# The seven products of a Strassen pair emitted ahead of their sums, the norm's scales behind the second pair, and attention's raw tiles in the ring of the output projection's weights

## The chip, the cores and the metric

The kernel runs on one core of a Trainium2 chip. The metric is the device time of one execution in microseconds (us). The kernel before takes 1793.49 us, the median of three runs (1792.94 to 1795.22). The engines named below are TensorE (PE, the matmuls; PEld is its weight load), VectorE (DVE), ScalarE (ACT), GpSimd (POOL) and SyncE (SP, which issues most of the DMAs).

## What is computed

One layer of a bidirectional hybrid encoder on a sequence of 1024 tokens with model width 1024, in float32. Cut to what matters here:

```python
h    = rms_norm(x, g1) @ W_in                  # one combined projection
cat  = concat[dilated-window attention (8 heads, 512 wide),
              bidirectional RWKV-7 (8 heads, 512 wide)]
x    = x + cat @ W_out                         # 1024 x 1024
h    = rms_norm(x, g2)                         # x / sqrt(mean(x^2) + 1e-6) * g2
x    = x + squared_relu(h @ W_up) @ W_down     # 1024 -> 4096 -> 1024
```

## The kernel before

**Matmuls.** Every large product is computed as three matmuls on rounded halves: `mm3` (L104-107) multiplies high by high (L105), high by low (L106) and low by high (L107) into one PSUM tile. `split_w` (L100-102) makes the halves of a raw tile: ACT casts it to the high half (L101, tiles `wuh`, `w2h`, `f`), and DVE subtracts that from the raw tile for the low half (L102, `wul`, `w2l`, `f`).

**Order.** The program is emitted in Python and a scheduler then sets the order of the instructions on each engine from its own model of their times, keeping the dependencies. So the order on an engine isn't the order of the code. Tiles come from pools with a fixed number of buffers; a tile that takes over a buffer waits until the last user of the one before is done. A DMA that SP issues blocks SP's later DMAs while it waits for its buffer.

**The end of the kernel** is `tail()` (L987-1237). Until about 1006 us attention's last pieces run beside it (`some`, L1013).

- *Output projection.* `w_out` (L1023) takes columns of W_out for a list of rows `ks` and an output block `c`, adds the product to `x1[c]` (L1038). First come rows 4 to 7 (the RWKV half and attention's last heads, L1041-1044) for all eight blocks, then row 0 (L1048), then rows 1 to 3 (L1062). Rows 0 to 2 are attention's results of earlier heads, which lie in device memory (`cat_dr`): `cat(k)` (L1018) loads one into a raw tile of 128x1024 (512 KB) and splits it into `f`. That raw tile comes from `raw4` (L1006), a ring of two buffers that the blocks of W_up use too, before and after. The weights' raw tiles `w2raw` (L1028) have a ring of three buffers in the pool `w0`.
- *MLP, up.* x1 is scaled by g2 only (`hraw`, L1071) and split into the seven right factors of a Strassen-Winograd scheme, `h11`, `h21`, `h22`, `hT1` to `hT4`, while rows 1 to 3 of `w_out` run. The norm's scale per token is not needed for these products, as it can be applied to their results. Two blocks of W_up make a pair (`up_unit`, L1157; 16 pairs): seven products "11", "21", "22", "T1" to "T4", each of 12 matmuls of 128x512 into a PSUM bank of its own (84 matmuls a pair; eight banks, pool `pu`). Their left factors come from `factors` (L1104): quarters of the raw blocks, or sums of them that POOL makes (`wus`, L1114, three buffers), each split into `wuh` and `wul` (four buffers). DVE makes the Winograd sums of the products (L1173, and L1195 for the first pair alone); `add` (L1168) emits each product together with its sum.
- *Norm.* `sums()` squares x1 on ACT (L1141, tile `sqt`) and adds the 16 squares up in `rep`, one half of the tokens on DVE, the other on POOL (L1142). `scales()` sums over the partitions with 16 small matmuls (`psr`, L1147), takes the square root on ACT (L110, with a load of the function table), the reciprocal on DVE (L111), spreads the result over the partitions with 8 matmuls (`psb`, L1153) and copies it back to `rep` on DVE (L1155).
- *Finish.* `finish(u)` (L1198) takes each of a pair's four results: ReLU and scale in one DVE instruction (L1200), square on POOL (L1201), and a DMA by POOL to device memory (`f_dr`, L1202).
- *MLP, down* (L1211-1237) reads `f_dr` back, splits it and adds to x1.

The first pair has an order of products of its own (11, 21, 22, T2, T3, T1, T4), with one more sum and one more copy (L1181-1184, L1193-1195); in the others it is 11, T2, T3, T1, 21, T4, 22. The code calls the first pair, the norm (`sums`, `scales`), `finish` of the first pair, and then pair after pair.

Of the kernel before, what the change touches and what calls it, by code (L numbers as in the profile page):

```python
# [16 lines left out]
P = 128  # L17
# [30 lines left out]
def tile_trunk(ctx: ExitStack, tc: tile.TileContext, xT, w_in, w_o, w_up, w_dn, vecs, w2w0, a2, g2, cst, att,  # L48
# [938 lines left out]
    def tail(pieces, left, rw, at, fps):  # L987
        with ExitStack() as st:
# [9 lines left out]
            o0 = ExitStack()  # L998
            c00 = o0.enter_context(tc.tile_pool(name="c00", bufs=1, side="right", reuse_waits="tile"))
            w0 = o0.enter_context(tc.tile_pool(name="w0", bufs=3, side="right", reuse_waits="tile"))  # L1000
# [17 lines left out]
            def cat(k):  # L1018
                raw = raw4(cat_dr[k].rearrange("p (k m) -> p k m", m=P)).rearrange("p k m -> p (k m)")
                for hf in range(2):  # L1020
                    split_w(raw[:, HS[hf]], fh[k][:, HS[hf]], fl[k][:, HS[hf]])

            def w_out(wp, ks, c):  # L1023
                ws = {}
                for i in range(0, len(ks), 3 if len(ks) == 3 else 2):
                    k = ks[i]
                    n = len(ks) if len(ks) < 4 else 2
                    raw = wp.tile([P, n, P], F32, name="w2raw", bufs=3)  # L1028
                    nc.sync.dma_start(raw, w_o[c][:, k:k + n])
                    w = [wp.tile([P, n, P], F32R, name=x) for x in ("w2h", "w2l")]  # L1030
# [10 lines left out]
            for c in range(NK):  # L1041
                nc.sync.dma_start(x1[c], xT[c * P:(c + 1) * P, :])
                w_out(w0, [4, 5, 6, 7], c)
                some(4)
# [59 lines left out]
            def factors(u):  # L1104
# [12 lines left out]
                if u == 0:  # L1117
                    yield halves(a12)
                s1 = summed(nc.gpsimd.tensor_add, a21, a22)
                s2 = summed(nc.gpsimd.tensor_sub, s1, a11)  # L1120
                if u == 0:
                    yield halves(summed(nc.gpsimd.tensor_sub, a12, s2))
# [3 lines left out]
                if u > 0:  # L1126
                    yield halves(a12)
                yield halves(a22)
                if u > 0:
                    yield halves(summed(nc.gpsimd.tensor_sub, a12, s2))  # L1130
# [25 lines left out]

            def up_unit(u):  # L1157
                w = factors(u)

                def prod(ps, q):  # L1160
                    wh, wl = next(w)
# [6 lines left out]
                def add(a, q, out):  # L1168

                    ps = acc()  # L1170
                    prod(ps, q)
                    for x, t in zip(a, out):
                        nc.vector.tensor_add(t, x, ps)  # L1173
                    return out
                ps = acc()
                prod(ps, "11")
                t1 = z("t", bufs=2)
                nc.scalar.copy(t1, ps)
                if u == 0:
                    z11, = add([t1], "21", [z("z")])  # L1180
# [157 lines left out]
```

## Time and profile before

| | |
|---|---|
| median of three runs | 1793.49 us |
| the profiled execution | 1798.4 us |
| its span, first to last instruction | 1796.5 us |
| PE busy, share of the span | 1630.6 us, 91% |
| DVE, ACT, POOL busy | 1030.1, 595.8, 420.4 us |
| mean granted TensorE clock | 0.932 |

The 1.9 us between the execution's time and its span lie around the first and the last instruction. Rows of a timeline give the start and the busy time of an instruction in us, the engine, the line, the operation, its output and input tiles with shapes, a count where like instructions follow each other, and in brackets the idle time of the engine just before and what ended it. Matmuls are pipelined, so the busy time of one is longer than the distance to the next.

### The profile page before, as it was taken

What the parts mean: (1) busy time and instruction counts of PE and PEld (TensorE: products, weight loads), DVE (VectorE), ACT (ScalarE), POOL (GpSimd) and SP (SyncE); (2) the same over time, 40 slices, a digit from 0 to 9 for tenths busy, and PEclk for the clock granted to TensorE, in tenths of its full rate; (3) what the DMA queues carried; (4) which work ended last, traced back from release to release, by engine and by line L of the source; (5) the groups of instructions that cost most, each with busy time, mean ns of one, the idle gap of its engine ahead of it and who ended that gap; (6) DMA issues with size and microseconds to landing.
All of it is one profiled execution on the core that took longest, in us unless ns stands there. A gap on an engine that the chain in (4) does not pass through costs nothing.

```text
span 1796.5 us, 29980 instructions
## 1 busy us (share of the span) xinstructions
PE 1630.6 (91%) x11720; PEld 1346.6 (75%) x11720; DVE 1030.1 (57%) x1949; ACT 595.8 (33%) x1092; POOL 420.4 (23%) x459
## 2 busy tenths in 40 slices
PE   7999978879869897989997997699999999999999
PEld 6777767767657777877786885588888778788887
DVE  6655658657554423565765577677877744242421
ACT  5534433344412213435464334322222222131310
POOL 3022121222200000221223125566666500000000
PEclk9999988889879997988997998799999999999999
DMA  7155787879874689997972501133333343241421
GB/s 220 43 141 133 155 165 171 172 170 186 193 172 124 184 207 219 263 270 200 248 195 85 197 24 36 53 110 119 106 110 113 123 147 117 71 140 47 141 94 47
DMA packets 338157, 256.66 MB, mean 143 GB/s; under 512 B 238912, under 2 KB 292048, under 8 KB 333920
## 3 DMA queue, kind: packets, MB, share of 16 engines
q1 hardware_dynamic: 301632, 212.60, 45.4%
q0 software_dynamic: 8704, 26.78, 4.9%
q10 hardware_dynamic: 27680, 15.38, 3.2%
q8 instruction: 92, 1.51, 0.4%
q14 instruction: 49, 0.40, 0.1%
HBM read 167.00 MB, written 87.69 MB: 142 GB/s over the span
## 4 chain that ended last, share of the span: by engine, by line
PE 63%; DMA 14%; DVE 11%; SPq 5%; ACT 4%; issue 3%; POOL 1%; ACTq 0%; DVEq 0%; POOLq 0%
PE ps L105 12%; PE ps L106 12%; PE ps L107 12%; PE ps_u L105 3%; PE ps_u L106 3%; PE ps_u L107 3%; DMA v_dr<-vn 2%; PE pvb L748 2%; PE psd L564 2%; PE psg L496 2%; DMA rec<-rec_dr 1%; DMA raw<-f_dr 1%; PE ps_pt L742 1%; DVE stmp L534 1%; DMA MP<-gd 1%
## 5 line engine op out<-in xcount | busy, mean ns | idle before, releaser
L105 PE MATMUL ps<-mh,wuh 128*128 128x512 f32 x512 | 199.6, 391 | 4.5 <-ACT mh L101 3.2
L106 PE MATMUL ps<-ml,wuh 128*128 128x512 f32 x512 | 199.8, 390 | 2.1 <-DVE ml L102 2.1
L107 PE MATMUL ps<-mh,wul 128*128 128x512 f32 x512 | 199.2, 389 | 0.0
L101 ACT CAST wuh<-raw 128x512 fp32r<-128x512 f32 x112 | 68.9, 622 | 284.7 <-PE ps L106 276.1
L105 PE MATMUL ps_u<-hh,wh 128*128 128x512 f32 x368 | 156.8, 426 | 3.5 <-DVE ur L308 3.5
L107 PE MATMUL ps_u<-hh,wl 128*128 128x512 f32 x368 | 149.9, 407 | 0.0
L106 PE MATMUL ps_u<-hl,wh 128*128 128x512 f32 x368 | 149.6, 407 | 0.0
L102 DVE TENSOR_TENSOR wul<-raw,wuh 128x512 fp32r<-128x512 f32 x112 | 104.7, 938 | 55.1 <-ACT wuh L101 53.6
L105 PEld LDWEIGHTS ps<-mh,wuh 128*128 128x128 f32 x512 | 96.1, 188 | 27.2 <-ACT mh L101 5.5
L106 PEld LDWEIGHTS ps<-ml,wuh 128*128 128x128 f32 x512 | 96.1, 188 | 23.7 <-DVE ml L102 3.8
L1235 DVE TENSOR_TENSOR x<-x,ps 128x512 f32<-128x512 f32 x64 | 43.8, 685 | 121.6 <-PE ps L107 121.6
L107 PEld LDWEIGHTS ps<-mh,wul 128*128 128x128 f32 x512 | 96.1, 188 | 19.9 <-DVE wul L102 0.4
L105 PEld LDWEIGHTS ps_u<-hh,wh 128*128 128x128 f32 x368 | 72.2, 196 | 20.4 <-DVE ur L308 4.3
L106 PEld LDWEIGHTS ps_u<-hl,wh 128*128 128x128 f32 x368 | 72.2, 196 | 16.7 <-issue 2.9
L107 PEld LDWEIGHTS ps_u<-hh,wl 128*128 128x128 f32 x368 | 71.5, 194 | 17.5 <-issue 1.4
L101 ACT CAST wuh<-wus 128x512 fp32r<-128x512 f32 x64 | 39.6, 622 | 130.1 <-PE ps L106 126.1
L102 DVE TENSOR_TENSOR ml<-raw,mh 128x512 fp32r<-128x512 f32 x64 | 42.5, 700 | 62.7 <-ACT mh L101 62.7
L496 PE MATMUL psg<-al,bk 64*128 64x128 f32 x512 | 56.6, 319 | 16.8 <-DVE G L501 8.6
L705 DVE CUSTOM_DVE_ANT_0 sb<-ps_s,bias 128x256 f32<-128x256 f32 (+1 forms) x136 | 50.0, 403 | 35.3 <-PE ps_pt L719 27.7
L1201 POOL TENSOR_TENSOR zz<-zz 128x512 f32<-128x512 f32 x48 | 57.3, 1195 | 42.0 <-DVE zz L1200 42.0
L496 PEld LDWEIGHTS psg<-al,bk 64*128 64x128 f32 x512 | 47.9, 217 | 24.5 <-issue 10.6
L102 DVE TENSOR_TENSOR wul<-wus,wuh 128x512 fp32r<-128x512 f32 x64 | 63.7, 998 | 4.4 <-ACT wuh L101 4.4
(410 smaller groups left out, 3985.9 us busy)
## 6 DMA issues: line engine op xcount, KB each, us to landing
rec<-rec_dr SPq DMA_DIRECT2D x32, 1152.0 KB, 10.1
raw<-in_w_up SPq DMA_DIRECT2D x32, 512.0 KB, 4.3
raw<-in_w_dn SPq DMA_DIRECT2D x32, 512.0 KB, 3.4
raw<-f_dr SPq DMA_DIRECT2D x32, 512.0 KB, 3.4
f_dr<-zz POOLq DMA_DIRECT2D x48, 256.0 KB, 2.5
raw<-in_w_in SPq DMA_DIRECT2D x46, 256.0 KB, 2.8
rec_dr<-al POOLq DMA_DIRECT2D x64, 128.0 KB, 4.1
rec_dr<-G SPq DMA_DIRECT2D x32, 256.0 KB, 4.4
```

The costliest lines, as they stand in the source:

```text
L101: nc.scalar.copy(hi, raw)
L102: nc.vector.tensor_sub(lo, raw, r2f(hi))
L105: nc.tensor.matmul(ps, lh, rh, start=start, stop=False)
L106: nc.tensor.matmul(ps, lh, rl, start=False, stop=False)
L107: nc.tensor.matmul(ps, ll, rh, start=False, stop=stop)
L496: nc.tensor.matmul(pss[h][:, c], bk[H[h], 4 * g + c, h:h + 2].rearrange("p a b -> p (a b)"), al[H[h], 4 * g + c].rearrange("p a b -> p (a ...
L534: nc.vector.tensor_mul(tmp[:, 0:s, 0:s], Tt[:, rs, rs], MP[:, rs, t:t + 1].rearrange("p a o -> p o a").to_broadcast([P, s, s]))
L564: nc.tensor.matmul(ps[H[h], c], L[H[h], c], R[H[h], c], start=True, stop=True)
L705: nc.vector.tensor_tensor_reduce(sb[rows, i, :n], ps[rows, i, cols], b[rows], -1.0, 3.0e38, ALU.add, ALU.min, O[rows, js][:, i, mc:mc + 1])
L748: nc.tensor.matmul(pv[:, i], pts[:, x, i * P:(i + 1) * P], vB[:, x * 4 + c], start=(x == 0), stop=(x == 1))
L1201: nc.gpsimd.tensor_mul(t, t, t)
L1235: nc.vector.tensor_add(x1[c][:, HS[hf]], x1[c][:, HS[hf]], ps)
```

## The change

In `tail()` three things are different.

1. `up_unit` becomes two functions. `products(u)` emits the seven products of a pair, each into its own PSUM tile; `together(ps)` emits the sums. All pairs take the products in the order 11, 21, T2, T3, T1, T4, 22. The special order of the first pair, its extra sum and its extra copy are gone.
2. The calls are: pair 0's products and sums, `sums()`, pair 1's products, `scales()`, `finish` of pair 0, the sums of pair 1 and their `finish`, then pairs 2 to 15.
3. `cat` loads four pieces of 128x256 for each of its three tiles, into buffers of `w2raw` in the pool `w0`, which has four now; the first two blocks of `w_out` over rows 4 to 7 take theirs from the pool `wp`, which rows 1 to 3 use later. The two buffers of `raw4` are left to W_up's blocks.

```diff
             def cat(k):
-                raw = raw4(cat_dr[k].rearrange("p (k m) -> p k m", m=P)).rearrange("p k m -> p (k m)")
-                for hf in range(2):
-                    split_w(raw[:, HS[hf]], fh[k][:, HS[hf]], fl[k][:, HS[hf]])
+                for i in range(4):
+                    sl = slice(i * 256, i * 256 + 256)
+                    raw = w0.tile([P, 2, P], F32, name="catr", tag="w2raw", bufs=4).rearrange("p k m -> p (k m)")
+                    nc.sync.dma_start(raw, cat_dr[k][:, sl])
+                    split_w(raw, fh[k][:, sl], fl[k][:, sl])
...
-                    raw = wp.tile([P, n, P], F32, name="w2raw", bufs=3)
+                    m = 2 if wp is w0 else 3
+                    raw = wp.tile([P, m, P], F32, name="w2raw", bufs=4 if wp is w0 else 3)[:, :n]
...
-                w_out(w0, [4, 5, 6, 7], c)
+                w_out(wp if c < 2 else w0, [4, 5, 6, 7], c)
...
                 yield halves(a11)
-                if u == 0:
-                    yield halves(a12)
+                yield halves(a12)
                 s1 = summed(nc.gpsimd.tensor_add, a21, a22)
                 s2 = summed(nc.gpsimd.tensor_sub, s1, a11)
-                if u == 0:
-                    yield halves(summed(nc.gpsimd.tensor_sub, a12, s2))
                 yield halves(s2)
                 yield halves(summed(nc.gpsimd.tensor_sub, a11, a21))
                 yield halves(s1)
-                if u > 0:
-                    yield halves(a12)
                 yield halves(a22)
-                if u > 0:
-                    yield halves(summed(nc.gpsimd.tensor_sub, a12, s2))
+                yield halves(summed(nc.gpsimd.tensor_sub, a12, s2))
...
+            def products(u):
+                out = []
+                for q, (wh, wl) in zip(("11", "21", "T2", "T3", "T1", "T4", "22"), factors(u)):
+                    ps = acc()
                     hi, lo = hq[q]
                     for j in range(4):
                         mm3(ps, wh[:, j], wl[:, j], hi[j], lo[j], j == 0, j == 3)
+                    out.append(ps)
+                return out
+
+            def together(ps):
...
+                nc.scalar.copy(t1, ps[0])
+                z11 = add(z("z"), t1, ps[1])
+                U2 = add(z("u", bufs=1), t1, ps[2])
+                U3 = add(t1, U2, ps[3])
+                z22 = add(z("z"), U3, ps[4])
+                V = add(z("z"), U2, ps[4])
+                z21 = add(U3, U3, ps[5])
+                z12 = add(V, V, ps[6])
+                return [(z11, 0, 0), (z22, 1, 1), (z21, 1, 0), (z12, 0, 1)]
...
-            first = up_unit(0)
+            outs = together(products(0))
             sums()
+            ps = products(1)
             scales()
-            finish(0, first)
-            for u in range(1, 16):
-                finish(u, up_unit(u))
+            finish(0, outs)
+            finish(1, together(ps))
+            for u in range(2, 16):
+                finish(u, together(products(u)))
```

**What the scheduler makes of it.** PE around the norm, before. `ps<-hT4` is the last product of pair 0, `ps<-h11` the first of pair 1:

```order
L105 MATMUL ps_11430<-hT4h_10909,wuh 128x512
L106 MATMUL ps_11430<-hT4l_10913,wuh 128x512
L107 MATMUL ps_11430<-hT4h_10909,wul 128x512
L1147 MATMUL psr_11493<-ct,rep_11273 128x2 x8
L1153 MATMUL psb_11504<-ct,rstd 128x128 x4
L1153 MATMUL psb_11510<-ct,rstd 128x128 x4
L105 MATMUL ps_11528<-h11h_10866,wuh 128x512
```

PE now, first at the end of pair 0 (`ps<-h22` of pair 0, then `ps<-h11` of pair 1), then 82 rows later at the end of pair 1 (`ps<-h22` of pair 1, then `ps<-h11` of pair 2):

```order
L105 MATMUL ps_11450<-h22h_10947,wuh 128x512
L106 MATMUL ps_11450<-h22l_10951,wuh 128x512
L107 MATMUL ps_11450<-h22h_10947,wul 128x512
L105 MATMUL ps_11528<-h11h_10896,wuh 128x512
L106 MATMUL ps_11528<-h11l_10900,wuh 128x512
```

```order
L106 MATMUL ps_11638<-h22l_10951,wuh 128x512
L107 MATMUL ps_11638<-h22h_10947,wul 128x512
L1144 MATMUL psr_11651<-ct,rep_11303 128x2 x8
L1150 MATMUL psb_11662<-ct,rstd 128x128 x4
L1150 MATMUL psb_11668<-ct,rstd 128x128 x4
L105 MATMUL ps_11719<-h11h_10896,wuh 128x512
```

So psr has moved from behind pair 0 to behind pair 1, with all 84 matmuls of pair 1 ahead of it.

DVE at the norm's additions (`rep`), before, from pair 0's sums to the reciprocal; and now:

```order
L1173 TENSOR_TENSOR zz<-zu,ps_11411 128x512
L102 TENSOR_TENSOR wul<-wus,wuh 128x512
L1142 TENSOR_TENSOR rep_11273<-rep_11273,sqt 128x512
L1195 TENSOR_TENSOR zz<-zz 128x512
L1173 TENSOR_TENSOR zt_11388<-zt_11388,ps_11430 128x512
L102 TENSOR_TENSOR wul<-wus,wuh 128x512
L1142 TENSOR_TENSOR rep_11273<-rep_11273,sqt 128x512 x6
L111 RECIPROCAL rstd<-rstd 128x8
```

```order
L1139 TENSOR_TENSOR rep_11303<-rep_11303,sqt 128x512
L1170 TENSOR_TENSOR zz<-zz,ps_11450 128x512
L1139 TENSOR_TENSOR rep_11303<-rep_11303,sqt 128x512
L102 TENSOR_TENSOR wul<-wus,wuh 128x512
L1139 TENSOR_TENSOR rep_11303<-rep_11303,sqt 128x512
L102 TENSOR_TENSOR wul<-wus,wuh 128x512
L1139 TENSOR_TENSOR rep_11303<-rep_11303,sqt 128x512
L102 TENSOR_TENSOR wul<-raw_11522,wuh 128x512
L1139 TENSOR_TENSOR rep_11303<-rep_11303,sqt 128x512
L1170 TENSOR_TENSOR zu<-zt,ps_11566 128x512
L1139 TENSOR_TENSOR rep_11303<-rep_11303,sqt 128x512
L102 TENSOR_TENSOR wul<-wus,wuh 128x512
```

Before, six of the additions follow each other with nothing between; now one stands between each two splits of pair 1's weights, and the last is ahead of the split of pair 1's seventh product.

SP where `cat` was loaded, before against now (`-` before, `+` now):

```order
-L1010 DMA raw_10712<-cat_dr_89 128x1024
-L1010 DMA raw_10718<-cat_dr_90 128x1024
+L1010 DMA raw_10952<-in_w_up 128x1024
+L1010 DMA raw_10954<-in_w_up 128x1024
+L896 DMA bon<-bon_dr 128x4x128
 L836 DMA cat_dr_91<-aT 128x512
-L896 DMA bon<-bon_dr 128x4x128
 L895 DMA gt<-g_dr 128x4x128
 L836 DMA cat_dr_91<-aT 128x448
 L836 DMA cat_dr_91<-aT 128x64
-L1010 DMA raw_10724<-cat_dr_91 128x1024
-L1010 DMA raw_10922<-in_w_up 128x1024
```

And where SP loads it now, between the weights of rows 4 to 7 and those of row 0 (128x128):

```order
L1032 DMA w2raw<-in_w_o 128x384 x4
L1032 DMA w2raw<-in_w_o 128x256 x5
L1022 DMA catr<-cat_dr_89 128x256 x4
L1022 DMA catr<-cat_dr_90 128x256 x4
L1022 DMA catr<-cat_dr_91 128x256 x4
L1032 DMA w2raw<-in_w_o 128x128 x8
```

The loads of attention's results have moved from ahead of the output projection to its middle, and W_up's first two blocks to the place where they were.

More of the change, by code (lines that the diff above doesn't have):

```diff
@@ L998, in tail @@
             o0 = ExitStack()
+            w0 = o0.enter_context(tc.tile_pool(name="w0", bufs=3, side="right", reuse_waits="tile"))
             c00 = o0.enter_context(tc.tile_pool(name="c00", bufs=1, side="right", reuse_waits="tile"))
-            w0 = o0.enter_context(tc.tile_pool(name="w0", bufs=3, side="right", reuse_waits="tile"))
             parts = [[(c13 if k else c00).tile([P, S], F32R, name=f"f{i}{k}") for k in range(4)] +
@@ L1027, in w_out @@
                     n = len(ks) if len(ks) < 4 else 2
-                    raw = wp.tile([P, n, P], F32, name="w2raw", bufs=3)
+                    m = 2 if wp is w0 else 3
+                    raw = wp.tile([P, m, P], F32, name="w2raw", bufs=4 if wp is w0 else 3)[:, :n]
                     nc.sync.dma_start(raw, w_o[c][:, k:k + n])
-                    w = [wp.tile([P, n, P], F32R, name=x) for x in ("w2h", "w2l")]
+                    w = [wp.tile([P, m, P], F32R, name=x)[:, :n] for x in ("w2h", "w2l")]
                     split_w(raw, *w)
@@ L1155, in scales @@
                     nc.vector.tensor_copy(rep[:, HS[hf]], psb)
[L1157 to L1161, printed above, removed]
+            def products(u):
+                out = []
+                for q, (wh, wl) in zip(("11", "21", "T2", "T3", "T1", "T4", "22"), factors(u)):
+                    ps = acc()
                     hi, lo = hq[q]
@@ L1164, in prod, with add @@
                         mm3(ps, wh[:, j], wl[:, j], hi[j], lo[j], j == 0, j == 3)
+                    out.append(ps)
+                return out
+            def together(ps):
                 def z(tag, **kw):
                     return zu.tile([P, 512], F32, name=f"z{tag}", tag=tag, **kw)
[L1168 to L1176, printed above, removed]
-                t1 = z("t", bufs=2)
-                nc.scalar.copy(t1, ps)
-                if u == 0:
-                    z11, = add([t1], "21", [z("z")])
-                    p3 = acc()
-                    prod(p3, "22")
-                    c3 = z("z")
-                    nc.scalar.copy(c3, p3)
-                U2, = add([t1], "T2", [z("u", bufs=1)])
-                U3, = add([U2], "T3", [z("t3", bufs=1)])
-                z22, V = add([U3, U2], "T1", [z("z"), z("z")])
-                if u > 0:
-                    z11, = add([t1], "21", [t1])
-                z21, = add([U3], "T4", [z("z") if u else U3])
-                if u > 0:
-                    z12, = add([V], "22", [V])
-                else:
-                    z12 = V
-                    nc.vector.tensor_add(V, V, c3)
-                return [(z22, 1, 1), (z11, 0, 0), (z21, 1, 0), (z12, 0, 1)]
+                def add(t, x, ps):
+                    nc.vector.tensor_add(t, x, ps)
+                    return t
+                t1 = z("t", bufs=2)
+                nc.scalar.copy(t1, ps[0])
[7 more added lines that the diff above has]
+                return [(z11, 0, 0), (z22, 1, 1), (z21, 1, 0), (z12, 0, 1)]
             def finish(u, outs):
```

## Prediction

> **What bounds the kernel now.** PE is busy for 91% of the span, so I looked for the stretch in which it isn't: first the stretches of 50 us around the two edits, from the table by windows. Its columns are the stretch, its length, busy time and instructions of PE, PEld, DVE, ACT and POOL, the granted clock, and the DMAs.
>
> ```profile
> 950.00:1000.00 50.00, 38.44 (x225) 33.40 (x225) 27.74 (x84) 24.09 (x52) 9.66 (x6) 0.76 0.33 108
> 1100.00:1150.00 50.00, 27.58 (x104) 22.89 (x103) 26.77 (x32) 17.75 (x30) 25.25 (x19) 0.69 0.07 21
> 1200.00:1400.00 200.00, 200.00 (x884) 165.62 (x883) 161.51 (x192) 51.35 (x85) 129.65 (x127) 1.00 0.31 108
> ```
>
> In the third row, the pairs' steady state, PE has no gap at full clock, with DVE at 81% and POOL at 65% beside it: nothing is to be had there. In the second, around the norm, PE works 27.58 of 50 us at a clock of 0.69. The first, attention's end, has a smaller hole. Which wait makes the hole at the norm, the waits of 1118 to 1150 say, and PE's timeline shows where it lies:
>
> ```profile
> PE psr L1147 <- DVE rep L1142: 16.1, 1, 16.1
> ACT sqt L1141 <- DVE rep L1142: 7.4, 6, 1.5
> ```
>
> ```profile
> 1106.35 0.80 PE L105 MATMUL ps<-h22h,wuh 128*128 128x512 f32 x1 [5.62 <-ACT wuh L101]
> 1112.51 0.40 PE L105 MATMUL ps<-hT2h,wuh 128*128 128x512 f32 x1
> 1122.07 0.39 PE L105 MATMUL ps<-hT4h,wuh 128*128 128x512 f32 x1
> 1138.96 3.85 PE L1147 MATMUL psr<-ct,rep 128*128 128x2 f32 x16 [16.06 <-DVE rep L1142]
> 1143.41 3.79 PE L1153 MATMUL psb<-ct,rstd 128*128 128x128 f32 x16 [0.60 <-DVE rstd L111]
> 1146.85 0.77 PE L105 MATMUL ps<-h11h,wuh 128*128 128x512 f32 x1
> 1150.94 0.39 PE L105 MATMUL ps<-hT2h,wuh 128*128 128x512 f32 x1
> 1167.27 0.39 PE L105 MATMUL ps<-h11h,wuh 128*128 128x512 f32 x1
> ```
>
> Pair 0 ends at 1122.07 plus three matmuls, 1122.75. PE then stands 16.06 us until the last addition of the norm, and pays for it afterwards:
>
> ```profile
> 1139.00:1147.20 8.20, 7.46 (x33) 7.29 (x34) 1.84 (x4) 2.03 (x3) 1.45 (x2) 0.50 0.01 2
> ```
>
> The clock is 0.50 all through psr and psb. Pair 1 starts at 1146.85 and takes 20.42 us until pair 2 at 1167.27; at full clock 72 matmuls take 1167.27 - 1150.94 = 16.33 us, 0.2268 each, so 84 take 19.05.
>
> **The norm behind pair 1: the main term.** By the order on PE, pair 1's 84 matmuls come between pair 0 and psr. I build PE's new times from these rows and from POOL's sums for the factors, two of pair 0 and three of pair 1:
>
> ```profile
> 1102.70 1.60 POOL L1114 TENSOR_TENSOR wus<-wus,raw 128x512 f32<-128x512 f32 x1
> 1104.38 1.26 POOL L1114 TENSOR_TENSOR wus<-raw,wus 128x512 f32<-128x512 f32 x1
> ...
> 1112.28 1.30 POOL L1114 TENSOR_TENSOR wus<-raw 128x512 f32<-128x512 f32 x1 [3.52 <-DMA raw<-in_w_up]
> 1113.66 1.62 POOL L1114 TENSOR_TENSOR wus<-wus,raw 128x512 f32<-128x512 f32 x1
> 1115.24 1.28 POOL L1114 TENSOR_TENSOR wus<-raw,raw 128x512 f32<-128x512 f32 x1
> ```
>
> 1. Pair 0's third product was "22", whose factor is the third POOL sum (ends 1105.64); it is T2 now, whose factor is the second (ends 1104.30). It starts 1.35 earlier, at 1105.00, and the five products left take 16.40 as before (1106.35 to 1122.75): pair 0 ends at 1121.40.
> 2. Pair 1 follows at once at full clock: 1121.40 + 19.05 = 1140.45. Its factors are there: POOL had made three of its sums by 1116.5.
> 3. psr: 3.85 at clock 0.50, half of it at full clock, 1.93: 1142.38.
> 4. Root and reciprocal. Before, the table load lay in the shadow of PE's wait:
>
> ```profile
> 1122.72 0.62 ACT L101 CAST wuh<-wus 128x512 fp32r<-128x512 f32 x1 [1.51 <-PE ps L106]
> ...
> 1139.50 1.28 ACT L110 ACT_TABLE_LOAD   x1
> 1142.85 0.27 ACT L110 ACTIVATE rstd<-psr,eps 128x8 f32<-128x8 f32 x1 [2.07 <-PE psr L1147]
> ```
>
> By ACT's order a cast of pair 2's fourth factor stands ahead of it now. The cast waits for its buffer until pair 1's last product ends, 1140.45; with 0.62 for it and 1.28 for the load ACT is ready at 1142.35, as psr ends. So the gap stays near the 0.60 of before; I take 0.65.
> 5. psb: from 1143.41 to 1146.85 it took 3.44 at half clock, 1.72 now. Pair 2 starts at 1142.38 + 0.65 + 1.72 = 1144.75.
>
> Pair 2 started at 1167.27: **22.5 us earlier**. Of these 16.1 are the idle time, 3.6 psr and psb at full clock, 1.4 pair 1's slow beginning, 1.35 pair 0's order.
>
> The 5.0 us of clock in it rest on rows: after the 16.06 us of idleness the clock was 0.50, and after 5.62 us of idleness it took from 1106.35 to 1112.51 until L105's spacing was short again. The Trainium skill ("TensorE: Matmul & The Clock Gate", What's actually happening) gives about 3.4 us of sustained work until full speed; a restart would then cost half of it, 1.7 us, and the change 3.3 less, 1774.6 as an estimate from that page. The trace's 6.2 us is longer, and the sum goes by the trace.
>
> **What must hide for that.** The squares and additions of the norm lie beside pair 1 now. Alone, they ran like this:
>
> ```profile
> 1120.58 0.62 ACT L1141 ACTIVATE sqt<-x 128x512 f32<-128x512 f32 x1
> 1136.23 1.15 ACT L1141 ACTIVATE sqt<-x 128x512 f32<-128x512 f32 x2 [1.47 <-DVE rep L1142]
> 1137.41 1.40 DVE L1142 TENSOR_TENSOR rep<-rep,sqt 128x512 f32<-128x512 f32 x1 [1.22 <-ACT sqt L1141]
> 1139.62 1.27 POOL L1142 TENSOR_TENSOR rep<-rep,sqt 128x512 f32<-128x512 f32 x1 [1.35 <-ACT sqt L1141]
> ```
>
> They took 1120.58 to 1140.89, though nothing else was to do: at the end a pair of additions every 2.61 us, each waiting for its square and the square for the buffer. psr needs the first half of `rep` at 1140.45 and the second at about 1141.4. At the old pace the DVE half (last addition 1137.41 + 1.40 = 1138.81) has 1.6 us to spare and the POOL half 0.5. Is there room for the old pace? The price of DVE's splits beside a busy POOL is in the steady state's groups:
>
> ```profile
> L102 DVE TENSOR_TENSOR wul<-wus,wuh 128x512 fp32r<-128x512 f32 x43 | 45.1, 1049 | 0.0
> L102 DVE TENSOR_TENSOR wul<-raw,wuh 128x512 fp32r<-128x512 f32 x32 | 41.3, 1292 | 1.3
> L1173 DVE TENSOR_TENSOR zz<-zt,ps 128x512 f32<-128x512 f32 x21 | 14.3, 680 | 14.3 <-PE ps L107 14.3
> ```
>
> From 1105.0 to 1140.45, 35.4 us, DVE has 12 splits (mean 1.15), 10 sums (0.68) and the 7 additions (1.40): 13.8 + 6.8 + 9.8 = 30.4 us, 86%. It fits, with 5 us left. So I take no wait of psr in the forecast; the bounds are 0 and the 8 us of the first rival. If that cover fails, the start of pair 2 moves by what is late.
>
> **After the norm** two pairs' results are finished close together. By the steady state's groups
>
> ```profile
> L1201 POOL TENSOR_TENSOR zz<-zz 128x512 f32<-128x512 f32 x33 | 39.2, 1189 | 21.0 <-DVE zz L1200 21.0
> L1202 POOL DMA_DIRECT2D f_dr<-zz x31 | 17.6, 569 | 3.3 <-POOL zz L1201 3.3
> ```
>
> POOL has 8 squares and 8 issues, 8 x (1.19 + 0.57) = 14.1 us, and four `wus` of 1.3 to 1.6, about 5.6: 19.7 against the 19.05 us of a pair. Until that is worked off, weights of pair 3 can be late; the wait is between 0 and some 3 us, and I take **1.0 lost**. From pair 3 on each pair has the same 18 DVE operations as before and seven of eight banks, and the down stage has its old order: nothing.
>
> **Attention's raw tiles.** Where `cat` was loaded, ACT stood, and behind it PE:
>
> ```profile
> 982.01 1.14 ACT L101 CAST f<-raw 128x512 fp32r<-128x512 f32 x2 [2.45 <-DMA raw<-cat_dr]
> 983.17 1.28 ACT L708 ACT_TABLE_LOAD   x1
> 985.46 0.47 PE L727 MATMUL pv<-vA,pts 128*128 128x65 f32 x2 [2.65 <-ACT OA L732]
> 1042.72 0.39 PE L105 MATMUL ps<-f,w2h 128*128 128x512 f32 x1
> ```
>
> The casts and the wait for their load leave this place, 2.45 + 1.14 of ACT; most of PE's 2.65 goes with them, 2.2 I reckon, of which 1.6 arrive at 1042.72, where row 0 begins (x's loads now stand ahead of the weights in SP's queue). Row 0 would begin at 1041.1. But now `cat` passes through the four buffers of the weights: from the split of block 6's weights on, five passes follow one another (block 7, three of `cat`, row 0's weights), each a DMA, a cast and a split:
>
> ```profile
> w2raw<-in_w_o SPq DMA_DIRECT2D x16, 128.0 KB, 4.2
> w2raw<-in_w_o SPq DMA_DIRECT2D x8, 64.0 KB, 1.8
> 1024.70 1.26 DVE L102 TENSOR_TENSOR w2l<-w2raw,w2h 128x256 fp32r<-128x256 f32 x1
> 1025.50 0.41 ACT L101 CAST w2h<-w2raw 128x256 fp32r<-128x256 f32 x1 [1.86 <-PE ps L106]
> 1029.07 0.42 DVE L102 TENSOR_TENSOR w2l<-w2raw,w2h 128x256 fp32r<-128x256 f32 x1 [0.76 <-ACT w2h L101]
> ```
>
> With a DMA of 1.8 to 4.2 us a pass takes 2.75 to 5.15 (0.12 between the steps), and from 1026 five end at 1039.8 to 1051.8. The 4.2 was measured beside x's eight loads of 512 KB, which are over by then; I take 2.2, a pass of 3.15, and 1041.8. Row 0 waits 0.7, and some more where pieces crowd: **0.7 gained**, between 2.65 gained and 9 lost.
>
> **The sum:** -22.5 + 1.0 - 0.7 = -22.2. The profiled execution, 1798.4 (span 1796.5 and 1.9 around it), would become 1776.2. It lies 4.9 above the median of the runs; carried over, 1793.49 - 22.2 = **1771.3 us**.
>
> **The rivals.**
>
> *The additions come late.* DVE's additions and splits both read two tiles of SBUF, beside POOL's. For it: in the steady state the splits' means are 1.05 and 1.29 against the 0.68 of the sums, which read one tile from PSUM, and the reserve of the POOL half is 0.5 us. If DVE and POOL exclude each other, seven more POOL additions put up to 7 x 1.27 = 8.9 us on DVE's 30.4: 39.3 against 35.4, 4 us late, and as much again where the splits of pair 1 wait behind them: 4 to 8 us, 1775 to 1779. The Trainium skill ("SBUF — State Buffer", Who interferes with whom) has this rule: VectorE with two SBUF inputs and a GpSimd instruction that reads SBUF exclude each other, and the second waits for the whole instruction. It speaks against the change; the splits' means beside a busy POOL agree with it. Against: those means have POOL at 65% in them already. Chance 0.14.
>
> *The ring of the weights.* The passes take 4.2 us of DMA as beside x: row 0 begins at 1051.8 rather than 1042.0, 9.8 lost, 1781; with half of that 1776. For it: nothing of a pass can overlap the next in the same buffer. Against: the 1.8 of the small loads. Chance 0.13.
>
> *The sums are late in every pair: slower.* Emitted behind all seven products, a pair's sums could hold seven of eight PSUM banks until its end, so that the next pair waits for DVE. It decides from 22.2 / 14 = 1.6 us for each of pairs 2 to 15; with 2 us it is 28 lost and 5.8 over: 1799. Against: the DVE order has the sums between the splits as before, and DVE's 19% of slack is 3.6 us a pair. Chance 0.04.
>
> *Nothing is hidden.* If pair 1's weights wait for the norm's work (POOL's sums stand behind its additions), PE stands as long inside pair 1, and only pair 0's order is left: 1791 to 1793. Against: those three sums of pair 1 are made by 1116.5, ahead of most additions. Chance 0.03.
>
> **The numbers.** The forecast has 0.66. The range of 1767 to 1780 takes in the forecast's bounds (3 better where attention's end gives its whole 2.65 and POOL costs nothing, with 1 for the clock) and both rivals but the end of the second. A measurement of this kernel can tell 0.2%, 3.6 us, from no change. Faster: 0.66 + 0.14 + 0.13 = 0.93; the same 0.03; slower 0.04.
>
> **What would show it.** Right: psr directly behind 84 matmuls without a wait over 1 us; clock 1.00 through psr and psb; pair 2 about 22 us earlier against row 0's first matmul. Wrong: a wait of psr for `rep`; PE waits in pairs 2 and 3 for `wuh`; over 2 us of wait at row 0 for `f` or `w2h`; gaps in the steady state.

## The result and the profile after

The changed kernel takes 1770.76 us, the median of four runs (1765.34 to 1773.15), against 1794.36 us of the kernel before on the same chip (four runs): ratio 0.9864, 95% interval 0.9839 to 0.9889. That is 23.6 us faster; 22.2 were forecast, and 1771.3 us. It was run once more as an experiment (1768.81 us, six runs), which gives a second profile.

The first profiled execution has a span of 1763.3 us, 33.2 less than the one before, 11 more than forecast. Where the two come apart is seen by setting the same places of the program beside each other. Four rows of the profile before that the prediction didn't show are needed for that: SP's issue of the first two 512 KB tiles at attention's end, the first matmul of pair 0, the first of the down stage and the last of all.

```profile
959.23 0.80 SPq L1010 DMA_DIRECT2D raw<-cat_dr  x2
...
1091.26 0.57 PE L105 MATMUL ps<-h11h,wuh 128*128 128x512 f32 x1 [3.75 <-ACT wuh L101]
...
1433.83 0.61 PE L105 MATMUL ps<-mh,wuh 128*128 128x512 f32 x2
...
1791.90 0.39 PE L107 MATMUL ps<-mh,wul 128*128 128x512 f32 x1
```

The changed kernel's timelines of SP and PE at the same places, with the third product of pair 0 (T2 now), the ends of pairs 0 and 1, psr and psb, and the first matmuls of pairs 2 and 3:

```profile
948.18 0.81 SPq L1010 DMA_DIRECT2D raw<-in_w_up  x2
...
984.31 0.55 PE L105 MATMUL ps<-rw,w2h 128*128 128x512 f32 x1 [0.66 <-ACT w2h L101]
...
1031.35 0.50 PE L105 MATMUL ps<-f,w2h 128*128 128x512 f32 x1 [0.71 <-ACT w2h L101]
...
1080.18 0.79 PE L105 MATMUL ps<-h11h,wuh 128*128 128x512 f32 x1 [3.75 <-ACT wuh L101]
...
1094.31 0.80 PE L105 MATMUL ps<-hT2h,wuh 128*128 128x512 f32 x1 [4.81 <-ACT wuh L101]
...
1111.15 0.39 PE L105 MATMUL ps<-h11h,wuh 128*128 128x512 f32 x1
...
1130.19 1.84 PE L1144 MATMUL psr<-ct,rep 128*128 128x2 f32 x16
1132.70 2.05 PE L1150 MATMUL psb<-ct,rstd 128*128 128x128 f32 x16 [0.67 <-DVE rstd L111]
1134.51 0.48 PE L105 MATMUL ps<-h11h,wuh 128*128 128x512 f32 x1
...
1154.22 0.39 PE L105 MATMUL ps<-h11h,wuh 128*128 128x512 f32 x1
...
1401.76 0.61 PE L105 MATMUL ps<-mh,wuh 128*128 128x512 f32 x2
...
1759.03 0.39 PE L107 MATMUL ps<-mh,wul 128*128 128x512 f32 x1
```

The differences between neighbouring rows give the stretches; the last column is the second profile of the changed kernel, from the same places of its timelines (pair 3 begins at 1186.31 before, by the PE timeline):

| stretch, us | before | changed | changed, again |
|---|---|---|---|
| start to the first two 512 KB tiles | 959.2 | 948.2 | 962.2 |
| from there to row 0 | 83.5 | 83.2 | 80.0 |
| row 0 to pair 0 | 48.5 | 48.8 | 48.9 |
| pair 0 to pair 3 | 95.05 | 74.04 | 73.76 |
| pair 3 to the down stage | 247.5 | 247.5 | 247.5 |
| down stage to the last matmul | 358.1 | 357.3 | 357.3 |

In the first stretch the two kernels issue the same instructions on PE and SP, and two executions of the changed one lie 14 us apart there: the additional 11 us belong to the execution and not to the change. The change is in the fourth stretch, 21.0 to 21.3 us, and a little in the second. The two profiles of the changed kernel agree in the fourth by parts that cancel: in the second one pair 0 is 1.46 us shorter (29.51 against 30.97), and pair 2 begins 1.41 later after psb's start (3.22 against 1.81), as psb is at half clock there.

The stretch that was the hole is full now. The table by windows of the changed kernel, around the norm:

```profile
1100.00:1150.00 50.00, 49.19 (x231) 40.73 (x230) 43.29 (x44) 20.52 (x35) 36.43 (x28) 0.99 0.19 66
```

PE works 49.19 of 50 us at a clock of 0.99, where it was 27.58 at 0.69. psr has no bracket, so PE had no wait ahead of it that the profile shows: the last additions on POOL and DVE, from their timelines, had ended ahead of psr's first matmul at 1130.19.

```profile
1127.19 1.81 POOL L1139 TENSOR_TENSOR rep<-rep,sqt 128x512 f32<-128x512 f32 x1
```

```profile
1123.15 1.01 DVE L1139 TENSOR_TENSOR rep<-rep,sqt 128x512 f32<-128x512 f32 x1
```

POOL's half is ready at 1129.00 and needed 0.9 us after 1130.19, by the second eight of psr's matmuls: 2.1 us to spare. DVE's half is ready at 1124.16, 6.0 us ahead. And ACT did what step 4 of the prediction said, the cast for pair 2 at pair 1's end and then the load of the table, beside psr:

```profile
1130.21 0.62 ACT L101 CAST wuh<-wus 128x512 fp32r<-128x512 f32 x1 [2.10 <-PE ps L106]
1130.85 1.28 ACT L110 ACT_TABLE_LOAD   x1
1132.15 0.27 ACT L110 ACTIVATE rstd<-psr,eps 128x8 f32<-128x8 f32 x1
```

### The profile page after: what moved, and what is told of

Same layout as the page of the kernel before. It is cut to its first block, busy times and chain, and to the rows that moved or that the text cites. A ratio compares the mean times of both kernels' runs of the same rounds, so it can differ in the third digit from the quotient of the medians.

```text
span 1763.3 us, 29984 instructions
## 1 busy us (share of the span) xinstructions
PE 1621.9 (92%) x11720; PEld 1336.9 (76%) x11720; DVE 1035.2 (59%) x1955; ACT 595.9 (34%) x1097; POOL 425.5 (24%) x459
## 5 line engine op out<-in xcount | busy, mean ns | idle before, releaser
L102 DVE TENSOR_TENSOR wul<-raw,wuh 128x512 fp32r<-128x512 f32 x112 | 101.1, 908 | 52.2 <-ACT wuh L101 52.2
L101 ACT CAST wuh<-wus 128x512 fp32r<-128x512 f32 x64 | 39.6, 622 | 127.8 <-PE ps L106 80.2
L102 DVE TENSOR_TENSOR wul<-wus,wuh 128x512 fp32r<-128x512 f32 x64 | 68.4, 1073 | 15.6 <-ACT wuh L101 15.5
```

Source lines behind the costliest of these rows:

```text
L101: nc.scalar.copy(hi, raw)
L102: nc.vector.tensor_sub(lo, raw, r2f(hi))
```

## The experiments

The theory was: the gain is the norm's work hidden beside pair 1 (idle time and clock), attention's tiles bring under 1 us, and emitting the sums apart costs nothing. The rivals were that attention's tiles bring the 11 us by which the profiles differ, that the sums apart matter by themselves, and that the norm is hidden only just. Ratios are against runs of the kernel before on the same chip, with 95% intervals.

**The pairs and the norm alone** (`e1_norm_only`): the changed kernel with attention's part as before.

```diff
...
-                for i in range(4):
-                    sl = slice(i * 256, i * 256 + 256)
-                    raw = w0.tile([P, 2, P], F32, name="catr", tag="w2raw", bufs=4).rearrange("p k m -> p (k m)")
-                    nc.sync.dma_start(raw, cat_dr[k][:, sl])
-                    split_w(raw, fh[k][:, sl], fl[k][:, sl])
+                raw = raw4(cat_dr[k].rearrange("p (k m) -> p k m", m=P)).rearrange("p k m -> p (k m)")
+                for hf in range(2):
+                    split_w(raw[:, HS[hf]], fh[k][:, HS[hf]], fl[k][:, HS[hf]])
...
-                w_out(wp if c < 2 else w0, [4, 5, 6, 7], c)
+                w_out(w0, [4, 5, 6, 7], c)
```

> The change to the pairs and the norm alone; attention's raw tiles stay in the ring of W_up's blocks as before. My theory: nearly the whole gain sits here, 21 to 22 us against the kernel before (ratio about 0.988), with pair 2 beginning some 21.7 us earlier after pair 0's first matmul (54.3 us instead of 76.0). Rival: attention's tiles bring a good part of the gain (the profiled span fell by 33 us, 11 more than the pairs account for); then this kernel gains 15 us or less.

Measured 0.9882 (0.9860 to 0.9903), 1772.33 us. In its PE timeline pair 0 to pair 2 takes 54.24 us, to pair 3 73.95: without the new place of attention's tiles the fourth stretch is as short as with it. The theory holds.

**Attention's tiles alone** (`e2_cat_only`): the same lines of the change, on the kernel before.

> Attention's raw tiles in the weights' ring alone; pairs and norm as before. My theory: 0 to 1 us gained, no difference that a measurement can tell (the two waits that it trades, 2.65 us of PE at attention's end against 0.7 us at row 0 and 0.7 us at the beginning of the output projection, with more of attention left beside it). Rival: 10 us gained, as the profiled executions differ by 11 us before this place is reached.

Measured 0.9988 (0.9970 to 1.0005): no difference that can be told, and 10 us are out. The profile is richer than the theory, though. From the first tiles to row 0 it took 79.81 us here. Over all profiles of this study it was 82.9 to 84.0 in the five kernels with the old place of the tiles, and in the eight with the new one five times 79.8 to 80.2 and three times 82.6 to 83.2. A window of 10 us shows what parts these, first of this kernel, then of the changed kernel's first profile (each from 20 us after the first tiles were issued):

```profile
973.98:983.98 10.00, 9.93 (x74) 9.43 (x73) 6.11 (x26) 7.86 (x19) 1.28 (x1) 0.84 0.58 210
```

```profile
968.18:978.18 10.00, 10.00 (x65) 9.72 (x64) 5.30 (x23) 7.15 (x17) 1.27 (x1) 0.69 0.50 189
```

PE is all but free of idle time in either (2.65 us before), but the clock came up at different moments, 0.84 against 0.69. Over the whole stretch the mean granted clock is 0.91 here and 0.88 in the changed kernel's first profile: 0.91 of 79.81 us and 0.88 of 83.17 are 72.6 and 73.2 us at full clock, so it is the clock that parts the two. So this part of the change is worth 0.3 to 3.7 us by the profile, as the clock falls.

This run also shows how much the clock alone moves the kernel before: from pair 0 on it has the same instructions, and pair 0 to pair 3 takes 93.55 us here against 95.05, as the clock came up earlier behind the norm (pair 1 takes 19.16 us in place of 20.42).

**Products and sums apart, norm as before** (`e3_apart_only`):

```diff
             outs = together(products(0))
             sums()
-            ps = products(1)
             scales()
             finish(0, outs)
-            finish(1, together(ps))
-            for u in range(2, 16):
+            for u in range(1, 16):
                 finish(u, together(products(u)))
```

> Products and sums emitted apart in the new order of products, but the norm's scales ahead of pair 1 as before, and attention's tiles as before. My theory: only pair 0's order counts, 1.0 to 1.4 us gained (the third product begins 14.1 instead of 15.1 us after the first), and PE still waits 16 us for the norm. Rival that the sums apart matter by themselves: pairs 2 to 15 change in length (19.04 us each before), 2 us or more of difference in all.

Measured 0.9974 (0.9958 to 0.9991), 4.7 us: neither theory's size. Pairs 2 to 15 take 19.04 us each, so the sums apart do nothing by themselves. But from pair 0 to pair 1 it is 50.76 us against 55.59, 4.8 less where 1.0 to 1.4 were expected, since PE waits shorter for the norm, whose POOL half is ready 44.82 us after pair 0's first matmul (1136.47) and before was ready after 49.63 (1140.89):

```profile
1134.44 1.87 PE L1141 MATMUL psr<-ct,rep 128*128 128x2 f32 x8 [11.61 <-DVE rep L1136]
1136.52 1.87 PE L1141 MATMUL psr<-ct,rep 128*128 128x2 f32 x8 [0.21 <-POOL rep L1136]
```

```profile
1135.20 1.27 POOL L1136 TENSOR_TENSOR rep<-rep,sqt 128x512 f32<-128x512 f32 x1 [1.35 <-ACT sqt L1135]
```

Two rows of ACT, of the kernel before and of this one, point to the cause:

```profile
1124.43 0.63 ACT L1141 ACTIVATE sqt<-x 128x512 f32<-128x512 f32 x1 [0.56 <-DVE zz L1195]
```

```profile
1117.74 1.15 ACT L1135 ACTIVATE sqt<-x 128x512 f32<-128x512 f32 x2
```

Squares and results share a ring of five buffers, and pair 0's old order kept one of them for the copy of product 22 until its extra sum (L1195) was done; a square waited for that. In the new order the squares begin 26.1 us after pair 0's first matmul, before it was 29.3 (1120.58 against 1091.26), and two of them run at once. The row shows one square's wait of 0.56 us for that buffer; that the buffer is also why the first square stands earlier in ACT's order isn't shown, as the scheduler sets that order.

**The clock alone** (`e4_warm`, `e4b_warm80`): matmuls that nobody reads in the kernel before, behind pair 0, on its last factor `wh` and `hi` (kept in `last` by a line in `prod`, cut here); 64 of them, then 80.

```diff
+            last = []
             first = up_unit(0)
             sums()
+            wh, hi = last
+            pf = acc("fill")
+            for i in range(64):
+                nc.tensor.matmul(pf, wh[:, i % 4], hi[i % 4], start=i == 0, stop=i == 63)
             scales()
```

> The kernel before, with 64 matmuls of 128x512 that nobody reads put between pair 0 and the norm's matmuls, on the last factor of pair 0: about 14.5 us of work in the 16 us in which PE waits. The wait for the norm stays as long; only the clock changes. My theory: the clock is 1.00 from the norm's matmuls on, which take 1.9 and 1.7 us instead of 3.85 and 3.44, and pair 1 takes 19.05 instead of 20.42: 5.0 us gained. Rival, that a restart costs half of some 3.4 us: 1.7 us gained. If the clock does nothing here: 0.

Measured 0.9997 (0.9981 to 1.0014). The 5 us did not come, and the PE timeline shows why:

```profile
1127.97 1.05 PE L1147 MATMUL psr<-ct,rep 128*128 128x2 f32 x8 [1.37 <-DVE rep L1142]
1130.03 1.40 PE L1147 MATMUL psr<-ct,rep 128*128 128x2 f32 x8 [1.01 <-POOL rep L1142]
1132.03 3.78 PE L1153 MATMUL psb<-ct,rstd 128*128 128x128 f32 x16 [0.60 <-DVE rstd L111]
```

psr ran at full clock, but with its waits 5.4 us passed from the last of the 64 to psb, in which PE had only psr's small matmuls, and psb is at half clock again. Pair 0 to pair 2 takes 73.83 us against 76.01. These 2.2 us are near the rival's 1.7, but not from the clock alone: psr began 1.4 us sooner after pair 0's first matmul than before (46.28 against 47.70; why isn't shown), and 0.8 are psr at full clock and a pair 1 of 20.06 us. With 80 this gap should close:

> As e4_warm with 80 matmuls that nobody reads in place of 64: in e4_warm they ended 1.4 us before the norm was ready, the small matmuls of psr followed with waits of 1.4 and 1.0 us, and psb was at half clock again after 5.4 us without a matmul of full size. With 80 they end some 2 us after the norm is ready, so psr and psb follow with 0.6 us between them. My theory that 2.5 us without large matmuls don't halve the clock but 5 us do, as the two profiles of the changed kernel and e4_warm suggest: psr 1.84, psb 1.8 and pair 1 in 19.1 to 19.7 us; from pair 0's first matmul to pair 2's 72.5 to 73.5 us, against 76.0 before and 73.8 in e4_warm, 5 us of clock less 2 us of overrun. Rival, that the clock falls by psr's small matmuls themselves: psb at 3.4 to 3.8 us again and no gain over e4_warm.

Measured 0.9985 (0.9967 to 1.0002), in the timeline:

```profile
1133.82 1.84 PE L1147 MATMUL psr<-ct,rep 128*128 128x2 f32 x16
1136.50 2.05 PE L1153 MATMUL psb<-ct,rstd 128*128 128x128 f32 x16 [0.84 <-DVE rstd L111]
```

psr, psb and pair 1 (19.17 us) are at full clock, and pair 0 to pair 2 takes 73.42 us against 76.01. The 80 matmuls lasted 18.1 us in a gap of 16.2, 1.9 too long; with that, the clock was worth 4.5 us, near the 5.0 of the prediction. Yet pair 2 comes only 2.6 us earlier, which the times can't tell from nothing: the wait for the norm stays, and matmuls that outlast it take back part of what the clock gives.

**Sums that can't begin before the pair's end** (`e5_sums_late`): in pairs 2 to 15 product 11, which every sum starts from, is the last.

```diff
-                yield halves(a11)
+                if u < 2:
+                    yield halves(a11)
...
+                if u > 1:
+                    yield halves(a11)
...
+                names = ("11", "21", "T2", "T3", "T1", "T4", "22")
-                for q, (wh, wl) in zip(("11", "21", "T2", "T3", "T1", "T4", "22"), factors(u)):
+                for q, (wh, wl) in zip(names if u < 2 else names[1:] + names[:1], factors(u)):
...
-                return out
+                return out if u < 2 else out[-1:] + out[:-1]
```

> The changed kernel, but in pairs 2 to 15 the product 11, on which every sum rests, comes last of the seven, so no sum can begin before the pair's end: this forces what the code's order suggests. My theory on why emitting the sums apart was harmless: the scheduler puts them between the splits anyhow, and even late sums cost little, as the banks come free in the order in which the next pair wants them and DVE has 19% of slack: at most 0.5 us for each of 14 pairs, 0 to 7 us over the changed kernel. Rival, the one of the prediction: 1.6 us and more for each pair, 22 us or more, no gain left.

Measured 0.9970 (0.9950 to 0.9990), 1787.26 us: 16.5 us over the changed kernel's median of 1770.76, and 18.5 over the 1768.81 of its later runs on this run's chip. Neither was right. PE waited around the pairs' ends, and most where the down stage begins; the waits of PE, first all of those between 1160 and 1390, then the longest at that transition:

```profile
PE ps L107 <- DVE wul L102: 3.9, 4, 1.8
PE ps L105 <- ACT zt L1177: 0.6, 1, 0.6
```

```profile
PE ps L106 <- DVE ml L102: 7.2, 1, 7.2
```

From pair 2's product 11 to the down stage it took 258.69 us where 13 pairs and a product at full clock are 13 x 19.04 + 2.72 = 250.2: 8.5 us, 0.65 a pair, and the down stage 6.5 longer, as it reads the results that come last. So late sums do make the next pair wait for DVE, at 0.65 a pair, but not as the rival had it: PE waits for the splits `wul`, which share DVE with the late sums, and only the 0.6 us behind `zt`, the copy of product 11, is a wait for a PSUM bank. These waits and one of 1.2 at the down stage's first matmul are 5.7 of the 8.5 us; the rest isn't taken apart here. In the changed kernel this doesn't happen: its pairs take 19.04 us and PE has no wait in them. DVE's timeline there has the sums between the splits, as the scheduler placed them.

**All additions on POOL, or all on DVE** (`e6_adds_pool`, `e7_adds_dve`), in the changed kernel; the diff is that of the first, the second has `nc.vector` in its place:

```diff
-                        (nc.gpsimd if hf else nc.vector).tensor_add(rep[:, sl], rep[:, sl], t)
+                        nc.gpsimd.tensor_add(rep[:, sl], rep[:, sl], t)
```

> The changed kernel with all 14 additions of the norm on POOL (seven on DVE and seven on POOL before). My theory: the norm is hidden with a reserve of only about 2 us on POOL (its last addition ended 1129.00, psr began 1130.19 and needed that half 0.9 later). With 14 additions and 4 sums for weights of 1.3 to 1.75 us from 1107.4 on, POOL ends near 1134.8; psr waits 4 to 5 us and the clock falls with it: 5 to 9 us over the changed kernel. If the cover were wide, nothing changes.

> The changed kernel with all 14 additions on DVE, none on POOL. If DVE and POOL shut each other out when both read two tiles (an addition took 0.68 to 1.78 us in the changed kernel), DVE's operations fall to 0.68 us when POOL is silent: 36 operations are some 25 us in the 35 there are, and the time stays as it is (0 to 1 us over). Rival: an addition costs DVE 1.40 us by itself, seven more are 9.8 us on some 30, and psr waits 4 to 5 us.

On POOL: 0.9908 (0.9874 to 0.9941), 1775.71 us, and pair 0 to pair 3 takes 79.28 us, 5.2 more than the changed kernel. psr waits:

```profile
1131.86 1.05 PE L1144 MATMUL psr<-ct,rep 128*128 128x2 f32 x8 [2.03 <-POOL rep L1139]
1133.08 1.05 PE L1144 MATMUL psr<-ct,rep 128*128 128x2 f32 x8 [0.17 <-POOL rep L1139]
1135.40 3.79 PE L1150 MATMUL psb<-ct,rstd 128*128 128x128 f32 x16 [1.27 <-DVE rstd L111]
```

The wait was 2.2 us, less than the 4 to 5 expected, and psb was at half clock besides (3.79 us). On DVE: 0.9892 (0.9865 to 0.9920), 1770.80 us, pair 0 to pair 3 73.95: nothing lost, although DVE has seven additions more. Its groups beside pair 1, first with all additions on DVE, then in the changed kernel (busy time, mean ns of one):

```profile
L1139 DVE TENSOR_TENSOR rep<-rep,sqt 128x512 f32<-128x512 f32 x14 | 12.1, 904 | 0.1
L102 DVE TENSOR_TENSOR wul<-wus,wuh 128x512 fp32r<-128x512 f32 x6 | 4.6, 768 | 1.6 <-ACT wuh L101 1.6
```

```profile
L1139 DVE TENSOR_TENSOR rep<-rep,sqt 128x512 f32<-128x512 f32 x7 | 9.6, 1377 | 0.2
L102 DVE TENSOR_TENSOR wul<-wus,wuh 128x512 fp32r<-128x512 f32 x6 | 6.2, 1048 | 0.0
```

Twice as many additions take 12.1 us in place of 9.6, and the splits beside them get shorter: of the 14 additions eleven took 0.68 us and three 1.60 to 1.79, each of the three beside a sum that POOL had in work. In the changed kernel two of seven took 1.01 and four 1.61 to 1.78. So what an addition costs DVE over 0.68 us, half of the 1.38, is the wait for POOL.

**The changed kernel again** (`after_again`), the same file.

> The changed kernel once more, for its spread and for a second profile. Both kernels run the same instructions up to attention's last loads; the place where SP issues the first two 512 KB tiles lay at 959.23, 954.08, 953.98, 959.48, 950.25 and 948.18 us in six profiles. My theory: that is the spread of executions and no part of the change; from that place on, this profile should again need 815 to 816 us to the end (837.3 before), and the median should lie 21 to 24 us under the kernel before. Rival: the prefix is shorter in the changed kernel by itself, then it is at about 948 here again.

Measured 0.9883 (0.9861 to 0.9905), 1768.81 us. The first tiles were issued at 962.24, the latest of all profiles, so the shorter prefix was the execution's. From there to the last matmul it took 807.4 us, against 810.9 in the first profile and 832.7 before. To the end of the span it is 811.7 where 815 to 816 were expected: the theory left out that the clock at attention's end moves the second stretch (80.0 against 83.2).

**A better order for pair 0** (`e8_t4_third`, `e9_t4_sums`): T4's factor is a raw block, so it goes third, in the place where PE waits 4.8 us for POOL; in the second kernel the squares are emitted ahead of pair 0's sums besides (the last piece of the diff).

```diff
...
+                if u == 0:
+                    yield halves(a22)
...
+                names = ("11", "21", "T2", "T3", "T1", "T4", "22")
-                for q, (wh, wl) in zip(("11", "21", "T2", "T3", "T1", "T4", "22"), factors(u)):
+                for q, (wh, wl) in zip(names if u else ("11", "21", "T4", "T2", "T3", "T1", "22"), factors(u)):
...
-            outs = together(products(0))
-            sums()
+            ps = products(0)
+            sums()
+            outs = together(ps)
```

> The changed kernel with pair 0 in the order 11, 21, T4, T2, T3, T1, 22. In the changed kernel PE waits 4.8 us ahead of T2 for POOL's second sum and then starts at half clock, while T4's factor is a raw block that is there. My theory: T4 fills 2.7 us of the wait, the rest is 1 to 2 us, too short for the clock to fall: 4 to 6 us gained over the changed kernel, from pair 0's first matmul to pair 3's first some 68 to 70 us in place of 74.0. The reserve of the norm decides: if its additions don't begin earlier with pair 0, psr waits and less is left. Rival: T4's right factor is the last that is split, T4 waits for it, and nothing is gained.

> As e8_t4_third, and the squares and additions of the norm emitted between pair 0's products and its sums, so that they begin some 10 us earlier on ACT, DVE and POOL. If the norm's reserve is used up in e8_t4_third (psr waits for rep there), this one is 1 to 4 us faster than it; if not, both take the same time, or this one is 1 to 3 us slower, as additions on POOL then stand ahead of the sums for pair 0's factors.

Measured 0.9897 (0.9872 to 0.9922) and 0.9880 (0.9855 to 0.9905): no gain over the changed kernel. In the first, T4 waits for its right factor, and the norm's end moves out; its PE timeline:

```profile
1098.87 0.50 PE L105 MATMUL ps<-hT4h,wuh 128*128 128x512 f32 x1 [1.84 <-ACT hT4h L1071]
1100.12 0.50 PE L106 MATMUL ps<-hT4l,wuh 128*128 128x512 f32 x1 [0.74 <-DVE hT4l L1072]
1102.18 0.80 PE L105 MATMUL ps<-hT2h,wuh 128*128 128x512 f32 x1 [1.32 <-ACT wuh L101]
...
1137.12 1.05 PE L1147 MATMUL psr<-ct,rep 128*128 128x2 f32 x8 [0.83 <-POOL rep L1142]
1141.70 3.78 PE L1153 MATMUL psb<-ct,rstd 128*128 128x128 f32 x16 [3.53 <-DVE rstd L111]
```

Pair 0 to pair 1 is 2.1 us shorter (28.90 against 30.97; 29.51 in the changed kernel's second profile), and 5.5 are lost from pair 1 to pair 2 (28.84 against 23.36; 24.91 in the second): psr's second half waits for POOL, and the reciprocal stands behind splits and sums on DVE. With earlier squares psr waits no more, but T2 waits longer for its factor, whose sum POOL had ready at 1101.69: ACT casts it behind the squares, and its low half stands behind additions on DVE. The rows of POOL, ACT and PE:

```profile
1100.41 1.28 POOL L1117 TENSOR_TENSOR wus<-wus,raw 128x512 f32<-128x512 f32 x1 [0.68 <-POOL wus L1117]
1103.58 0.61 ACT L101 CAST wuh<-wus 128x512 fp32r<-128x512 f32 x1
1104.24 0.79 PE L105 MATMUL ps<-hT2h,wuh 128*128 128x512 f32 x1 [3.18 <-ACT wuh L101]
1107.33 0.79 PE L107 MATMUL ps<-hT2h,wul 128*128 128x512 f32 x1 [1.87 <-DVE wul L102]
```

Pair 0 to pair 3 takes 77.33 us in the first and 76.33 in the second, both above 74.0. The theory was right that T4 shortens pair 0 and wrong on the sum, as the norm's end decides. By the stretch the changed kernel's order is the best of the three; the times don't tell them apart.

## Why the prediction was right

1. *Pair 0's order, 1.35 us.* In the profile 0.96 to the third product (14.13 against 15.09 us after the first matmul), of which 0.4 were given back to the end of pair 0: 30.97 to pair 1 against 31.49 to pair 0's end before. The term was too large by 0.8. What it missed is that the new order also starts the squares earlier, by the freed buffer as far as the rows show: the norm is ready 4.8 us sooner in the experiment with its old place (`e3_apart_only`). As the whole wait for the norm vanished anyway, that didn't enter the sum, but point 6 rests on it.
2. *Pair 1 at once, at full clock: 19.05.* 1111.15 to 1130.19 is 19.04.
3. *psr 1.93, gap 0.65, psb 1.72.* 1.84, 0.67 and 1.81. In the second profile psb is at half clock, 3.22 from its start to pair 2: full clock there depends on the execution.
4. *Pair 2 earlier by 22.5.* Pair 0's first matmul to pair 2's is 54.33 us against 76.01: 21.7.
5. *1.0 lost behind the norm.* 0.67, pair 2 takes 19.71 us. The cause was named wrongly: not POOL and not in pair 3, which takes 19.04. The loss lies in pair 2 in steps too short for a bracket. The largest is in product T1, whose `wul` DVE had ready at 1146.18: the matmul that reads it began 0.53 us behind the one before, at 1146.24, where 0.23 is the rule.
6. *The reserve of the norm.* Forecast 0.5 us for POOL's half and 1.6 for DVE's at the old pace; they were 2.1 and 6.0. But the pace wasn't the old one, and here the forecast was lucky. After pair 0's first matmul POOL's half was ready at 49.63 us before, at 44.82 with the new order and PE waiting for it (`e3_apart_only`), and at 48.82 beside pair 1. So pair 1's work cost the norm 4.0 us, which the forecast put at nothing (it had counted DVE's load and not POOL's), and the earlier squares, which it didn't know of, gave 4.8. With the squares as late as before, POOL's half would by these figures have come at some 53.6, 2.7 us after the 50.9 at which psr needs it: an estimate, as no run has both. That it is POOL's half that ends last was right: with all additions there psr waits, with all on DVE it doesn't.
7. *DVE and POOL shut each other out.* That rule, of the first rival, is borne out by the additions, 0.68 us or 1.0 to 1.8 beside POOL, and the size came near: the rival had the norm 4 us late, and pair 1's work cost POOL's half 4.0 us and DVE's 1.2 (how much of it by this rule isn't split off). Its consequence, that psr waits, didn't come, as the earlier squares made room for it. The Trainium skill ("SBUF — State Buffer", Who interferes with whom) says so of a VectorE instruction with two SBUF inputs and a GpSimd instruction that reads SBUF, and the two runs agree with it: the sums, which read one tile from PSUM, take 0.67 to 0.69 us in both, whatever POOL does.
8. *Attention's tiles, 0.7.* Row 0 waited 0.71 us, as forecast (0.42 in the second profile), and the output projection's beginning 0.66, which the sum didn't have. The forecast's 2.2 and 1.6 us were judged and not worked out. The size was 0.3 in one profile of the changed kernel and 3.5 in the other; the bound of 2.65 was too low, as it left out the clock. Before, it was 0.50 from 985.74 to 992.56, behind PE's wait of 2.65 us; in the second profile of the changed kernel it stayed at 1.00 from 985.49 to row 0.

So terms 4 and 5 make 21.0 of profile, where 21.5 were forecast, or 19.5 against `e2_cat_only`, where the clock came up earlier behind the norm. The medians' 23.6 us, and 21.4 in the second set of runs, are that and some of the eighth. How much of it is the eighth stays open within its interval (0.9970 to 1.0005). The mechanism was right: PE's work of pair 1 in the place of its wait, at full clock. That the time came within 0.6 us of the forecast is luck: the two sets of runs lie 2 us apart, and single terms missed by 0.8 to 2.8 us.

## What to carry to other kernels

A serial chain in front of a pipeline is hidden by giving the pipeline one more stage's work that doesn't need the chain; the price is set by buffers, so count who holds the ring that both draw from, and by the engine whose part of the chain ends last. What such a wait costs is more than its length, as the matmuls behind it run at half clock, and work put into the wait only to keep the clock up didn't pay here. Two profiles are compared place by place from the last point at which the programs are the same, and not by their spans.

## What the runs showed of the hardware

- *The clock can fall behind a gap of 2.5 us, and where the gap lies decides.* Between the last large matmul (of pair 1, in `e4b_warm80` of the 80) and psb lay 2.51 to 2.74 us with psr's 16 small matmuls in them. psb took 2.05 us behind gaps of 2.51, 2.52, 2.52 and 2.68 us, but 3.57 behind 2.65, 3.64 behind 2.74, and 3.15 behind 2.51. The second profile of the changed kernel:

```profile
1139.59 1.84 PE L1144 MATMUL psr<-ct,rep 128*128 128x2 f32 x16
1142.24 3.57 PE L1150 MATMUL psb<-ct,rstd 128*128 128x128 f32 x16 [0.80 <-DVE rstd L111]
```

The length of the gap alone doesn't decide, and that 2.5 us don't halve the clock, as expected for `e4b_warm80`, isn't so. The moments at which the granted clock changes lie on a grid of 3.41 us within each profile: in this one at 1142.50 and 1145.91, in the changed kernel's first one at 1100.67, of which 1131.39 is nine steps on. Windows cut on the grid, two of the second profile, then two of the first:

```profile
1139.09:1142.50 3.41, 2.61 (x21) 2.40 (x21) 3.09 (x6) 2.17 (x3) 0.35 (x1) 1.00 0.00 0
1142.50:1145.91 3.41, 3.41 (x17) 3.41 (x17) 1.74 (x3) 0.00 (x0) 1.19 (x2) 0.50 0.44 125
...
1127.98:1131.39 3.41, 3.41 (x23) 3.02 (x21) 2.36 (x4) 1.29 (x3) 1.02 (x1) 1.00 0.00 0
1131.39:1134.80 3.41, 2.74 (x23) 2.63 (x23) 1.81 (x5) 1.01 (x2) 1.26 (x1) 1.00 0.16 22
```

In the second profile the whole gap, 1139.59 to 1142.24, lies inside one window, and the clock is halved in the next. In the first, 1131.39 cuts the gap 1130.19 to 1132.70 in two, and the clock stays. So it is in all seven profiles: the three falls have the gap inside one window, which leaves 0.67 to 0.90 us in it for matmuls other than psr's; the four others have it cut, with 1.35 us or more in each window. The Trainium skill ("TensorE: Matmul & The Clock Gate", What's actually happening) speaks of a free-running window of about 3.4 us, which agrees with the grid; that it takes a whole idle window of this length doesn't agree with the three falls, as PE had matmuls in each of those windows.

- *Executions of the same instructions differ by up to 14 us* ahead of the place where the kernels part: the first two tiles were issued between 948.18 and 962.24 in the profiles, and the medians of the kernel before in four sets of runs are 1790.2 to 1794.4. Differences under some 3 us are read here from stretches of the profile and not from the times.
